# A two-layer encoder on one core: other order of the first loads, squares of x placed after its copies, group sums by transposes, the last sum in two runs

## The chip, the cores and the metric

The kernel runs on one core of a Trainium2 chip. Its engines are TensorE (PE, with PEld for its weight loads), VectorE (DVE), ScalarE (ACT), GpSimd (POOL) and SyncE (SP), each with its own in-order queue; sixteen DMA engines move data between memory and the chip. The metric is the device time of one execution in microseconds (us), lower is better. The median of three runs before the change is 617.97 us (617.78 to 618.43).

## The reference, cut to what matters

Two layers work on x of 256 tokens by 1024 features, all in float32. A layer is a mixer and then a channel part:

```python
h = rms_norm(x, n1)
proj = h @ w_in_l                      # 1024 x 2560: q, k, v of three kinds of heads
out_a = neighbourhood_attention(...)   # 4 heads
out_d = dilated_window_attention(...)  # 6 heads
out_c = gqa_block_attention(...)       # 6 heads, 2 of keys and values
mix = concat(rms_norm(out_a), rms_norm(out_d), rms_norm(out_c))
x = x + mix @ w_out_l
h = rms_norm(x, n2)
g, u = split(h @ w_gu)                 # 2 x 2816
x = x + (gelu(conv3(g)) * u) @ w_dn
```

`rms_norm` divides a row by the root of its mean square. The division is by one number for a token, so it can be taken after a product with weights.

## The kernel before, in words

**Numbers.** A float32 product is taken in three products of a faster format. An operand is split into a high part (a cast, by ScalarE) and a low part (what the cast left, by VectorE); `mm3` (line 610) adds high x high, high x low and low x high in PSUM. In profile names `wp_raw` is a piece of weights as loaded, `wp_hi` and `wp_lo` its parts, `act_hT` the turned x with its two parts side by side, `psa` and `psw` PSUM tiles of one bank each, four of either kind, and `act_s2k` a scratch tile with many uses. x lives in `const_x` (128 partitions, two halves t of 128 tokens, 1024 features); a block of x is 128 features of both halves.

**Weights.** They are streamed in units of at most 1 MB through four raw tiles and two pairs of part tiles (`load`, 561; `split`, 584; `unit`, 599). The first projection, "dq", needs two units of 768 KB: unit 0 holds feature blocks 0 to 3, unit 1 blocks 4 to 7. Unit 0 is loaded in four slices of one block, mixed with x, the gains of the norms, and the identity that transposes need; the list `START` (45) gives the queue and the order of these loads. Unit 1 is loaded in two halves, later units in one piece each.

**The start.** `gains_T` (506) transposes the gains. `split(0)` casts unit 0's slices. `split_T` (623) transposes x by TensorE, two blocks to a PSUM tile, and for each block ScalarE writes the high part times the gain and VectorE the low part. Then come the projections (802); `mean_squares` (647) has ScalarE square x in four pieces of 128 x 512 with the sum over a row as a by-product, and GpSimd turn the sums into the mean and its root. The mean is first needed when the heads of "dq" are normed (875), once "dq" is summed. Matmuls on a constant tile (`warm`, 512 to 524) fill TensorE's time before the weights are there.

**Group sums.** Each of the three groups of heads is normed over its features, which after attention lie on the partitions. `mixed` (1032) adds up the squares in a 128 x 256 tile; `group_rstd` (1047) sums them over the partitions by a matmul with a column of ones, copies the 128 x 2 result to SBUF and takes the root. `out_projections` (826) has VectorE scale the product with `w_out` by it and add it to x. There are three such sums a layer, after the sixth head, the twelfth and the last one.

**The end.** `down` (1308) adds the steps of the last product into four PSUM tiles `dacc[t][h]` of 128 x 512, one for each half of tokens and of features. The last two steps are taken together: for each of the four tiles, 12 matmuls of 512 columns, 6 a step. VectorE then scales each tile, adds it to x, and in the last layer SyncE stores the piece.

**What sets the order.** The program does not run in the order in which it is written. All operations are first recorded by `Plan` (220) with what they depend on. `order` (301) then simulates the engines with a price for each operation (`cost`, 414), a price for handing over from engine to engine, and one for loads (lines 384 to 392), and always takes the operation that can begin first; of two that can begin at once, the one of lower rank. The rank is the place in the text plus what `later(n)` adds. `not_before(engine)` (245) makes operations depend on the last one recorded so far on that engine. The engines' queues are written in the order so found. For dependencies a PSUM tile counts as a whole bank whatever part is used (`footprint`, 130):

```python
if self.tile.pool.psum:
    return (0, P, ((0, BANK),))
```

All operations are issued from line 411, so the profile's groups have to be told apart by their tiles.

Of the kernel before, what the change touches and what calls it, by code (L numbers as in the profile page):

```python
# [11 lines left out]
F32 = mybir.dt.float32  # L12
# [33 lines left out]
    ("act", "x", (0, 1)), ("sync", "g", 0), ("act", "x", (1, 1)), ("sync", "ident", 0), ("sync", "w", 0),  # L46
# [8 lines left out]

SPLIT_LATER, TURN_LATER, MIX_LATER, PREP_LATER = 50, 100, 100, 30
# [163 lines left out]
class Plan:  # L220
# [80 lines left out]
    def order(self):  # L301
# [49 lines left out]
        while len(done) < len(ops):  # L351
# [102 lines left out]
def encoder_kernel(  # L454
# [76 lines left out]
    ones = const.tile([P, 1], F32, tag="ones", name="ones")  # L531
    nc.gpsimd.memset(ones, 1.0)
# [257 lines left out]
    for l in range(DEPTH):  # L790
# [60 lines left out]
        me, rx = mean_squares(f"n1{l}")  # L851
# [195 lines left out]
        def group_rstd(gi):  # L1047
# [259 lines left out]

        def down(steps):
            ws = [unit() for _ in steps]
            for h in range(2):  # L1310
                hs = slice(h * 512, (h + 1) * 512)
                for t in range(NT):
                    c = slice(t * P, (t + 1) * P)
                    for s, (wh, wl) in zip(steps, ws):
# [104 lines left out]
```

## Time and profile before

| | |
|---|---|
| median of three runs | 617.97 us (617.78 to 618.43) |
| the profiled execution's own time | 617.81 us |
| its span, from first to last instruction | 616.0 us |
| TensorE, VectorE, ScalarE busy | 98%, 79%, 70% of the span |
| granted TensorE clock, mean | 0.999 |
| moved by DMA | 104.66 MB, 170 GB/s in the mean |

The span is what the trace covers; the time holds 1.8 us more around it. A row of instructions gives its start and its length, the engine, the line, the operation, output and inputs with their shapes, how many it merges, and in brackets how long the engine was idle before and what released it. A row of a group gives count, total busy time, mean in ns, and the idle time before. The row of a chain of waits gives the start, the length and what ran. Matmuls are pipelined: one row's length includes the time through the array, so the pace is read from start to start. ScalarE's `ACTIVATION_READ_ACCUMULATOR` is the second half of a square with a sum.

### The profile page before, as it was taken

To read this page: it belongs to the slowest core of one execution; us is meant where nothing else is said; L and a number is where in the kernel's file an instruction comes from. 1 tells how busy PE (TensorE), PEld (TensorE's weight loads), DVE (VectorE), ACT (ScalarE), POOL (GpSimd) and SP (SyncE) were. 2 spreads that over 40 slices of the span, in tenths; PEclk is the share of its full clock that TensorE was granted. 3 is DMA by queue.
4 is the path that set the end of the run, shared out by engine and by line. 5 is a ranking of instruction groups with operands and counts; after the bars stand their busy time and mean duration, and the time that the engine had idled before them with its cause. 6 is when DMAs were issued, how large, how long until landed. Compare 5 with 4: busy or idle time off the path is not lost.

```text
span 616.0 us, 9844 instructions
## 1 busy us (share of the span) xinstructions
PE 606.0 (98%) x3496; PEld 524.8 (85%) x3496; DVE 485.8 (79%) x1000; ACT 428.8 (70%) x1064; POOL 77.4 (13%) x125
## 2 busy tenths in 40 slices
PE   8999999999999999999999999999999999999997
PEld 6999878888888888888899989887888888888886
DVE  4898988897877877777867798979877777777775
ACT  6888989686566565556588899897756565566551
POOL 2731230211500000000023212112000000000000
PEclk9999999999999999999999999999999999999999
DMA  8894311755596555655444632127575555555501
GB/s 284 274 291 146 103 38 37 245 195 197 183 231 222 178 197 204 199 169 162 155 148 150 233 104 86 34 73 243 182 238 173 191 205 186 169 192 204 168 40 68
DMA packets 81617, 104.66 MB, mean 170 GB/s; under 512 B 9480, under 2 KB 69224, under 8 KB 81568
## 3 DMA queue, kind: packets, MB, share of 16 engines
q1 hardware_dynamic: 81024, 103.78, 52.0%
q8 instruction: 27, 0.44, 0.3%
q10 hardware_dynamic: 544, 0.26, 0.1%
q14 instruction: 22, 0.18, 0.1%
HBM read 102.54 MB, written 1.49 MB: 169 GB/s over the span
## 4 chain that ended last, share of the span: by engine, by line
PE 93%; ACT 3%; DVE 2%; DMA 1%; issue 1%; SPq 0%; ACTq 0%; DVEq 0%
PE psw_w L411 49%; PE psa_a L411 44%; ACT act_s2k L411 2%; DMA wp_raw<-in_w_in_dram 1%; DVE act_hT L411 1%; DVE wp_lo L411 1%; DVE const_x L411 0%; ACT wp_hi L411 0%; ACT act_hT L411 0%; ACT act_ch L411 0%; SPq L411 0%; DVE act_cl L411 0%; DVE act_z L411 0%; ACT const_v L411 0%; DVE small_nm L411 0%
## 5 line engine op out<-in xcount | busy, mean ns | idle before, releaser
L411 DVE TENSOR_TENSOR wp_lo<-wp_raw,wp_hi 128x512 fp32r<-128x512 f32 (+2 forms) x348 | 243.9, 729 | 49.7 <-ACT wp_hi L411 47.8
L411 PE MATMUL psw_w<-act_hT,wp_hi 128*128 128x512 f32 x704 | 247.6, 397 | 2.0 <-DVE act_hT L411 2.0
L411 ACT CAST wp_hi<-wp_raw 128x512 fp32r<-128x512 f32 (+2 forms) x348 | 212.7, 660 | 29.3 <-PE psw_w L411 15.6
L411 PE MATMUL psw_w<-act_hT,wp_lo 128*128 128x256 f32 x704 | 195.7, 279 | 0.0
L411 PEld LDWEIGHTS psw_w<-act_hT,wp_hi 128*128 128x128 f32 x704 | 131.8, 188 | 34.1 <-DVE act_hT L411 3.2
L411 PEld LDWEIGHTS psw_w<-act_hT,wp_lo 128*128 128x128 f32 x704 | 132.6, 188 | 1.2
L411 PE MATMUL psa_a<-wp_hi,act_hT 128*128 128x384 f32 (+2 forms) x448 | 113.1, 333 | 1.3 <-ACT act_hT L411 1.2
L411 ACT COPY act_s2k<-psw_w 128x256 f32<-128x256 f32 x88 | 32.3, 372 | 80.2 <-PE psw_w L411 80.2
L411 PEld LDWEIGHTS psa_a<-wp_hi,act_hT 128*128 128x128 f32 x448 | 77.9, 189 | 4.5 <-ACT act_hT L411 1.6
L411 PE MATMUL psa_a<-wp_lo,act_hT 128*128 128x384 f32 (+2 forms) x224 | 74.6, 334 | 0.0
L411 PE MATMUL psa_a<-wp_lo,act_ch 128*128 128x512 f32 x176 | 69.5, 395 | 0.0
L411 PE MATMUL psa_a<-wp_hi,act_ch 128*128 128x512 f32 x176 | 69.3, 394 | 0.0
L411 PE MATMUL psa_a<-wp_hi,act_cl 128*128 128x512 f32 x176 | 66.1, 394 | 0.0
L411 DVE TENSOR_TENSOR act_s2k<-psw_w,act_s2k 128x256 f32<-128x256 f32 x88 | 36.8, 422 | 32.4 <-ACT act_s2k L411 31.9
L411 PEld LDWEIGHTS psa_a<-wp_lo,act_hT 128*128 128x128 f32 x224 | 42.2, 189 | 1.9 <-DVE wp_lo L411 1.0
L411 PEld LDWEIGHTS psa_a<-wp_hi,act_cl 128*128 128x128 f32 x176 | 33.2, 188 | 7.7
L411 PEld LDWEIGHTS psa_a<-wp_hi,act_ch 128*128 128x128 f32 x176 | 33.1, 188 | 7.8
L411 PEld LDWEIGHTS psa_a<-wp_lo,act_ch 128*128 128x128 f32 x176 | 33.1, 188 | 6.9
L411 DVE SCALAR_TENSOR_TENSOR act_s2k<-act_s2k,act_cw,act_s2k 128x255 f32<-128x255 f32 x88 | 36.7, 476 | 1.4 <-ACT act_s2k L411 1.3
L411 POOL TENSOR_TENSOR small_rstd<-small_ms,const_mh 128x6 f32<-128x6 f32 (+2 forms) x26 | 32.0, 1232 | 2.2
L411 ACT ACTIVATE act_s2k<-act_s2k,act_cw 128x256 f32<-128x256 f32 x44 | 24.1, 595 | 11.6 <-DVE act_s2k L411 11.6
L411 PE MATMUL psw_w<-act_ch,const_v 128*128 128x256 f32 x128 | 28.5, 287 | 1.6 <-ACT act_s2k L411 1.1
(109 smaller groups left out, 754.3 us busy)
## 6 DMA issues: line engine op xcount, KB each, us to landing
wp_raw<-in_w_gate_up_dram SPq DMA_DIRECT2D x44, 1024.0 KB, 5.0
wp_raw<-in_w_down_dram SPq DMA_DIRECT2D x22, 1024.0 KB, 4.8
wp_raw<-in_w_in_dram SPq DMA_DIRECT2D x14, 768.0 KB, 5.9
wp_raw<-in_w_in_dram SPq DMA_DIRECT2D x8, 1024.0 KB, 5.9
wp_raw<-in_w_out_dram SPq DMA_DIRECT2D x8, 768.0 KB, 4.3
wp_raw<-in_w_out_dram SPq DMA_DIRECT2D x4, 512.0 KB, 3.8
act_nab<-dram_scr SPq DMA_DIRECT2D x4, 448.0 KB, 7.0
out_dram<-const_x SPq DMA_DIRECT2D x4, 256.0 KB, 2.0
```

Source lines behind the costliest of these rows:

```text
L411: getattr(o.engine.real, o.method)(*map(real, o.args), **{k: real(v) for k, v in o.kw.items()})
```

## The change

The list of the first loads is altered: the gains of the first norm come on ScalarE's queue in place of x's block 1, which goes to SyncE's queue behind the first slice of weights. x is copied in runs of 1, 1, 2 and 4 blocks in the first layer, the first run ahead of `split(0)`, whose operations depend on it. The four squares of the first layer depend on the last of those copies and have 50 added to their rank. The planner's prices for the first loads are altered. `group_rstd` transposes the two 128 x 128 halves of the squares and sums over the columns, instead of a product with ones. In the last layer the last of the four tiles is summed in two runs of 256 columns, with two sums and two stores. The second layer's start keeps its order of operations.

```diff
 START = [
-    ("act", "x", (0, 1)), ("sync", "g", 0), ("act", "x", (1, 1)), ("sync", "ident", 0), ("sync", "w", 0),
+    ("act", "x", (0, 1)), ("act", "g", 0), ("sync", "ident", 0), ("sync", "w", 0), ("sync", "x", (1, 1)),
     ("sync", "w", 1), ("sync", "x", (2, 2)), ("sync", "w", 2), ("sync", "w", 3), ("sync", "x", (4, 2)),
     ("sync", "x", (6, 2)), ("sync", "g", 1), ("sync", "g", 2),
 ]
+SQUARES_LATER = 50
...
+    def last_of(self, engine):
+        return max(i for i, o in enumerate(self.ops) if o.engine.name == engine)
-    def not_before(self, engine):
-        self.behind = max(i for i, o in enumerate(self.ops) if o.engine.name == engine)
+    def not_before(self, engine, at=None):
+        self.behind = self.last_of(engine) if at is None else at
...
-                end = max(end + 900, wires.get(ring, 0.0))
+                early = i < self.first_loads
+                end = max(end + (350 if early else 900), wires.get(ring, 0.0))
                 shared = 0.0
-                if i < self.first_loads:
-                    shared = o.size if ring == "ACT" else min(o.size, 120 * max(0.0, wires.get("ACT", 0.0) - end))
-                wires[ring] = end + shared / 120 + (o.size - shared) / (280 if i < self.first_loads else 360)
-                end = wires[ring] + 900
+                if early:
+                    shared = o.size if ring == "ACT" else min(o.size, 110 * max(0.0, wires.get("ACT", 0.0) - end))
+                wires[ring] = end + shared / (150 if ring == "ACT" else 110) + (o.size - shared) / (280 if early else 360)
+                end = wires[ring] + (1700 if early else 900)
...
-    ones = const.tile([P, 1], F32, tag="ones", name="ones")
-    nc.gpsimd.memset(ones, 1.0)
...
-    def mean_squares(name):
+    def mean_squares(name, behind=None):
...
-                nc.scalar.activation(
-                    junk, xs[:, t, h * 512 : (h + 1) * 512], AF.Square, accum_out=ss[:, t, h : h + 1]
-                )
+                with nc.not_before("ACT", behind) if behind else nullcontext():
+                    nc.scalar.activation(
+                        junk, xs[:, t, h * 512 : (h + 1) * 512], AF.Square, accum_out=ss[:, t, h : h + 1]
+                    )
...
-            split(0)
-        for h in range(2):
-            split_T(halves(h), hT_hi, hT_lo, 4 * h, gains[:, 0, l, 4 * h : 4 * h + 4], f"n1{l}{h}")
+        for b, n in [(0, 1), (1, 1), (2, 2), (4, 4)] if l == 0 else [(0, 4), (4, 4)]:
+            srcs = [xs[:, t, b * P : (b + n) * P] for t in range(NT)]
+            split_T(srcs, hT_hi, hT_lo, b, gains[:, 0, l, b : b + n], f"n1{l}{b}")
+            if l + b == 0:
+                with nc.not_before("ACT"):
+                    split(0)
+        turned_x = nc.last_of("ACT")
...
-        me, rx = mean_squares(f"n1{l}")
+        with nc.later(SQUARES_LATER if l == 0 else 0):
+            me, rx = mean_squares(f"n1{l}", turned_x if l == 0 else None)
...
-                nc.tensor.matmul(
-                    ps[:, t : t + 1], hold["sq", gi][:, t * P : (t + 1) * P], ones, start=True, stop=True
-                )
+                cols = slice(t * P, (t + 1) * P)
+                nc.tensor.transpose(ps[:, cols], hold["sq", gi][:, cols], ident)
-            nc.vector.tensor_copy(ss, ps[:, :NT])
+            nc.vector.reduce_sum(ss, ps[:, :S].rearrange("p (t d) -> p t d", d=P), axis=AX.X)
...
+        ends = whole = [(h, t, 0, 512) for h in range(2) for t in range(NT)]
+        if l == DEPTH - 1:
+            ends = whole[:-1] + [(1, NT - 1, 0, 256), (1, NT - 1, 256, 256)]
+
         def down(steps):
             ws = [unit() for _ in steps]
+            for h, t, c0, n in ends if STEPS - 1 in steps else whole:
+                hs, os = slice(h * 512 + c0, h * 512 + c0 + n), slice(c0, c0 + n)
...
+                            dacc[t][h][:, os], ch[:, j, c], cl[:, j, c], wh[:, j, hs], wl[:, j, hs],
+                            s == 0 and j == 0, s == STEPS - 1 and j == 1 and c0 + n == 512,
...
+        for h, t, c0, n in ends:
+            hs = slice(h * 512 + c0, h * 512 + c0 + n)
+            nc.vector.scalar_tensor_tensor(
+                xs[:, t, hs], dacc[t][h][:, c0 : c0 + n], r2[:, t : t + 1], xs[:, t, hs], ALU.mult, ALU.add
+            )
+            if l == DEPTH - 1:
+                nc.sync.dma_start(ov[:, t, hs], xs[:, t, hs])
```

More of the change, by code (lines that the diff above doesn't have):

```diff
@@ L2 @@
 import re
-from contextlib import ExitStack, contextmanager
+from contextlib import ExitStack, contextmanager, nullcontext
 import numpy as np
@@ L1306, in up @@
             ready[s] = (ch, cl)
+        ends = whole = [(h, t, 0, 512) for h in range(2) for t in range(NT)]
+        if l == DEPTH - 1:
+            ends = whole[:-1] + [(1, NT - 1, 0, 256), (1, NT - 1, 256, 256)]
         def down(steps):
             ws = [unit() for _ in steps]
[L1310 to L1314, printed above, removed]
-                        ch, cl = ready[s]
-                        for j in range(2):
-                            mm3(
-                                dacc[t][h], ch[:, j, c], cl[:, j, c], wh[:, j, hs], wl[:, j, hs],
-                                s == 0 and j == 0, s == STEPS - 1 and j == 1,
-                            )
+            for h, t, c0, n in ends if STEPS - 1 in steps else whole:
+                hs, os = slice(h * 512 + c0, h * 512 + c0 + n), slice(c0, c0 + n)
+                c = slice(t * P, (t + 1) * P)
+                for s, (wh, wl) in zip(steps, ws):
+                    ch, cl = ready[s]
+                    for j in range(2):
+                        mm3(
+                            dacc[t][h][:, os], ch[:, j, c], cl[:, j, c], wh[:, j, hs], wl[:, j, hs],
+                            s == 0 and j == 0, s == STEPS - 1 and j == 1 and c0 + n == 512,
+                        )
         last = []
```

9 lines of the change are left out of this document (1 added, 8 removed).

## The prediction

> **What bounds the kernel now.** I read the page first, then a table of stages, then the chain of waits, and last the single instructions of the places that the diff touches. From the page, the span, the busy shares and the chain by engine:
>
> ```profile
> span 616.0 us, 9844 instructions
> PE 606.0 (98%) x3496; PEld 524.8 (85%) x3496; DVE 485.8 (79%) x1000; ACT 428.8 (70%) x1064; POOL 77.4 (13%) x125
> ...
> PE 93%; ACT 3%; DVE 2%; DMA 1%; issue 1%; SPq 0%; ACTq 0%; DVEq 0%
> ```
>
> TensorE makes up 93% of the chain, so an edit can pay only where PE waits or by taking work off PE. Three stages (start:end, length, busy time of PE, PEld, DVE, ACT, POOL, granted clock, DMA share, GB/s) show where it waits; the rest is nearly full:
>
> ```profile
> 0.00:15.00 15.00, 12.69 (x74) 9.90 (x75) 6.74 (x17) 9.93 (x25) 3.96 (x14) 1.00 0.86 281
> 80.00:130.00 50.00, 47.40 (x304) 39.70 (x303) 42.86 (x102) 41.06 (x113) 12.85 (x17) 1.00 0.32 104
> 400.00:450.00 50.00, 48.51 (x287) 40.78 (x286) 43.15 (x96) 39.33 (x92) 6.47 (x10) 1.00 0.52 171
> ```
>
> PE idles 2.31 us in the first, 2.60 and 1.49 in the two around the ends of the layers' attention. The change reaches all three, and the last microseconds.
>
> **The start as it is.** The chain of waits of the first 30 us, cut to what matters, and two stretches, the second and third of the first projection's matmuls alone:
>
> ```profile
> 1.63 4.46 DMA wp_raw<-in_w_in_dram
> ...
> 6.11 0.52 ACT wp_hi L411
> ...
> 8.01 1.32 ACT act_s2k L411 x4
> 9.33 0.82 ACT wp_hi L411 x2
> ...
> 11.61 0.61 ACT act_s2k L411 x2
> ...
> 12.95 0.61 ACT act_s2k L411 x2
> ...
> 14.01 14.85 PE psa_a L411 x81
> ```
>
> ```profile
> 6.00:14.00 8.00, 6.84 (x42) 5.80 (x42) 5.57 (x14) 7.65 (x22) 0.27 (x2) 1.00 1.03 349
> ...
> 7.00:14.00 7.00, 5.24 (x24) 1.00 1.03 350
> 14.00:18.50 4.50, 4.49 (x24) 1.00 0.98 272
> ```
>
> The first weights land at 6.09. From 6 to 14 ScalarE is busy 7.65 of 8.00 us and sets the pace: it casts four slices of weights, copies x's eight blocks, and squares x in between (the act_s2k rows), 1.32 + 0.61 + 0.61 = 2.54 us on the chain. By 14.0 PE has done 24 of the first projection's 48 matmuls; from 14.01 it is dense, the other 24 taking 4.49, 0.187 each.
>
> **Part 1, the loads.** SyncE's first issues, and the GB/s of the first 8 us in forty slices:
>
> ```profile
> 1.18 0.41 SPq L411 DMA_DIRECT2D const_ident<-in_c_ident_dram  x1
> 1.63 0.91 SPq L411 DMA_DIRECT2D wp_raw<-in_w_in_dram  x2
> ```
>
> ```profile
> GB/s 0 0 0 0 0 0 0 0 15 115 253 246 310 233 241 159 197 187 200 261 307 346 269 243 261 243 202 279 264 289 315 320 382 359 358 376 361 374 374 387
> ```
>
> x's blocks 0 and 1, the gains, the identity and the first slice (131 + 131 + 8 + 66 + 197 KB) are 533 KB; the row adds up to that at 4.2 us, and the slice lands 1.9 us later. With block 1 behind it, 402 KB go ahead, reached at 3.7, and the slice takes the identity's slot, 0.45 us sooner. Estimate: landing at 5.5, the first matmul at 6.3 (7.04 now). Block 1 lands as the last of the 533 KB, at 6.1, just before its use. Block 0's copy, now in a PSUM tile of its own and ahead of the casts, waits only for block 0 and the gains, and the gains now come on ScalarE's queue, which issues two loads as before: nothing. SyncE's queue loses one issue (the gains) and takes one (block 1), so from blocks 2 and 3 on the bytes and slots ahead are the same and nothing behind lands earlier.
>
> **Part 2, the squares** go behind the last copy. ScalarE's copies and casts of this stretch are then done at 13.43 - 2.54 = 10.9 by ScalarE's own work, and two other things are late next: arrivals and PE itself.
>
> ```profile
> DMA packets 2158, 2.84 MB, mean 355 GB/s; under 512 B 128, under 2 KB 2158, under 8 KB 2158
> ```
>
> ```profile
> 13.43 3.01 ACT L411 CAST wp_hi<-wp_raw 128x384 fp32r<-128x384 f32 x7
> 18.33 0.28 POOL L411 TENSOR_SCALAR small_ms<-small_ss,small_he 128x6 f32<-128x6 f32 x1 [2.77 <-ACT act_s2k L411]
> 22.98 1.76 ACT L411 CAST wp_hi<-wp_raw 128x384 fp32r<-128x384 f32 x4 [1.55 <-DMA wp_raw<-in_w_in_dram]
> ...
> 14.00:23.00 9.00, 8.99 (x50) 8.70 (x51) 6.87 (x16) 7.07 (x36) 5.81 (x10) 1.00 1.03 325
> ```
>
> x, the first unit, the identity and the gains are 1.05 + 0.79 + 0.07 + 0.02 = 1.93 MB; the second unit's halves (0.39 each) end at 2.32 and 2.71. 1.75 MB have moved at 8.0 (the sum of the row above), then 355 GB/s (the first row here, 8 to 16 us); with the 1.9 us they land at 11.5 and 12.6. PE went dense 0.58 after the cast of 13.43 began, so arrivals allow 12.1. But PE must first do 24 matmuls and 16 transposes from 6.3 on: 24 x 0.187 + 16 x 0.11 (0.11 is worked out in part 3) = 6.3, so 12.6. I take 12.6: **-1.4 us**. Bounds: -1.9 by arrivals, and +0.8 if the squares come before the casts (x lands 1.9 us after 1.93 MB, at 10.4; its last copies end at about 11.7, an estimate, and 11.7 + 2.54 is 0.8 behind 13.43).
>
> The squares' 2.54 us need a cover: between 14 and 23 ScalarE works 7.07 of 9.00, so 1.93 are free, and the stretch begins 1.4 earlier; 0.8 remain. Queued behind them are the casts for the second projection and the sums of the first one's heads; and GpSimd's mean of x, which had 2.77 us to spare before it was used, loses about that much. The cast at 22.98 waits for a transfer and does not move; PE needs it at 14.01 + 72 x 0.183 = 27.2 now, 25.8 then, so this cover holds.
>
> **Part 3, the group sums**, six of them. Old sum and next transpose, two runs of transposes, the two kinds of read, and a wait on the read:
>
> ```profile
> 419.05 0.50 PE L411 MATMUL psw_w<-const_ones,act_sqm 128*128 128x1 f32 x4
> 419.41 0.27 PE L411 MATMUL psw_w<-const_ident,act_s2k 88*128 88x88 f32 x1
> ...
> 121.14 0.38 PE L411 MATMUL psw_w<-const_ident,const_x 128*128 128x128 f32 x2
> ...
> 121.83 0.82 PE L411 MATMUL psw_w<-const_ident,const_x 128*128 128x128 f32 x6
> ...
> 90.60 0.77 PEld L411 LDWEIGHTS psw_w<-act_kc,act_qc 64*128 64x128 f32 x12 [0.36 <-DVE small_ss L411]
> ```
>
> ```profile
> L411 DVE TENSOR_REDUCE small_nm<-psw_w 128x1 f32<-128x256 f32 x24 | 8.7, 416 | 2.5 <-PE psw_w L411 1.8 <-ACT act_s2k L411 0.6
> ...
> L411 DVE COPY small_ss<-psw_w 128x2 f32<-128x2 f32 x6 | 0.9, 155 | 0.5 <-PE psw_w L411 0.3
> ```
>
> The four old records take 0.36 from start to start; transposes (0.82 - 0.38) / 4 = 0.11 each, two 0.22. PE saves 0.14 a sum. The read grows from 0.155 to about 0.416 (nearest row: a reduction over as many columns), +0.26, so the result is 0.12 later. At the sum of 90 us PE waits for that read: +0.12. The last group of each layer feeds the sum into x that PE's transposes wait for: the saving goes into that wait, 0. The other three: -0.42. Together **-0.3 us**; bounds 6 x -0.14 = -0.84, and 6 x +0.26 = +1.6. The memset of the ones, ahead of all work on GpSimd, is worth nothing.
>
> **Part 4, the last sum.** TensorE's pace by width, a case of a PSUM bank written in two parts, two widths of the sum, and the end:
>
> ```profile
> 143.33 5.56 PE psa_a L411 x24
> 148.90 11.29 PE psw_w L411 x64
> ...
> 380.85 0.97 PE L411 MATMUL psw_w<-act_kc,act_qc 64*128 64x256 f32 x12
> 381.86 0.76 DVE L411 TENSOR_REDUCE small_nm<-psw_w 128x1 f32<-128x256 f32 x2 [0.26 <-PE psw_w L411]
> ...
> 123.58 1.65 DVE L411 SCALAR_TENSOR_TENSOR act_hT<-psw_w,const_gains,act_hT 128x256 fp32r<-128x256 f32 x4
> ...
> 612.41 0.75 DVE L411 SCALAR_TENSOR_TENSOR const_x<-psa_a,small_rx,const_x 128x512 f32<-128x512 f32 x1 [0.65 <-PE psa_a L411]
> ...
> 613.19 0.33 SPq L411 DMA_DIRECT2D out_dram<-const_x  x1
> ```
>
> ```profile
> GB/s 0 0 0 0 0 0 0 0 0 0 0 0 358 369 369 215 215 379 410 287 21 0 0 328 379 379 226 0 0 0 338 379 369 226 0 0 0 0 0 0
> ```
>
> 512 columns take 5.56 / 24 = 0.232; the run of 64 is half 512 and half 256 wide, so 256 take (11.29 - 32 x 0.232) / 32 = 0.12: splitting is free on PE (24 x 0.12 against 12 x 0.232, +0.1). Does the first half's sum start before the second half's matmuls end? The reduction at 381.86 reads columns whose six matmuls are the first of the twelve, and starts after all twelve: the program orders by whole banks. So both sums follow PE's end: 2 x 0.41 = 0.83 (1.65 / 4) instead of 0.75. The last issue is 0.08 later, its data, four slices of 0.2 us now (608 us + the row's slices), half as long: -0.35; **-0.25 us**. Bounds: -0.65 if the halves are tracked apart (0.75 - 0.41 and the 0.35), +0.15 if 1 KB rows move at half the rate.
> The Trainium skill (PSUM — Partial Sum Buffer, "PSUM bank collisions raise a hardware error") says the same of any engine pair: guard by bank, a different address in the bank still collides. The trace agrees (0.26 us of wait at 381.86); by address the end would be 0.4 better, by bank -0.25.
>
> **Part 5, the planner's new load prices** move no work themselves, but the whole order is written anew from them: valued at 0; this is the last rival.
>
> **The sum** against the profiled execution's own 617.81 (span 616.0 and 1.8 around it; the runs' median is 617.97): 617.81 - 1.4 - 0.3 - 0.25 = **615.9**.
>
> **Rivals.**
> (1) All at its better bound: -1.9 - 0.84 - 0.65 gives 614.4. For it: the stages are full of PE work. Against: the wait at 381.86.
> (2) The start's gain is taken back: ScalarE, with 0.8 us left, hands over the second projection's casts late, or the landing at 22.98 comes later because transfers fill the queue (DMA share 1.03 to 23 us). Leaves -0.3 of the start: 617.81 - 0.3 - 0.3 - 0.25 = 617.0. Against: 1.4 us between landing and use.
> (3) PE's clock falls in the gap between the warm-up and the first matmul:
>
> ```profile
> 0.98 3.25 PE L411 MATMUL psw_w<-const_warm 128*128 128x256 bf16 x15 [0.98 <-POOL const_warm L411]
> ```
>
> Those first fifteen took 0.217 each, against 0.12 for 256 columns later. A second such stretch loses 3.25 x (1 - 0.12 / 0.217) = 1.45: 617.3. Against: the gap shrinks, and the granted clock is 1.00 throughout.
> The Trainium skill (TensorE: Matmul & The Clock Gate, "What's actually happening") has the clock halve after one idle window of about 3.4 us; no gap here comes near, so by that rule it stays up.
> (4) Slower: the new order costs in the attention. Place: the stages 80:130 and 400:450, where PE already idles 4.09 us; a group's read or a head's copy queued one place worse stops PE, whose queue is in order. Doubled, 617.81 - 1.95 + 4.09 = 620.0; it decides from 6.04 us of idle time there, twice the present one being 8.18. For it: every order after the start depends on times that move. Against: durations and hand-overs of that part are priced as before, and the chain is PE's, unbroken, for 81 matmuls from 14.01.
>
> **How the numbers follow.** Forecast 0.58 (its own range 614.9 to 616.8), rivals 0.09, 0.18, 0.04 and 0.11. A measurement of this kernel can tell 0.2%, 1.2 us, from no change. Faster by more than that is below 616.7: most of the forecast, (1), and some of (2), 0.69; within it the rest of (2), (3) and the edges, 0.21; slower 0.10. The range 614.4 to 617.6 takes in (1), (2) and (3) and leaves (4) out.
>
> **What would show it.** Right: the first weight cast near 5.5; no squares among the copies; PE dense at 12.6; PE idle under 1.2 us between 7 and 14; six pairs of transposes with reductions near 0.42; two final sums after PE's end, the last issue at the same distance from it. Wrong: casts of the second unit behind squares, a PE wait on wp_hi or wp_lo between 14 and 30, or more than 6 us idle in the two attention stages.

## The result and the profile after

The changed kernel takes **622.93 us** (median of 4 runs, 622.65 to 623.44) against 617.88 us (617.77 to 618.43) before: ratio 1.008, 95% interval 1.0068 to 1.0091. It is slower by 5 us. The forecast was 615.9 us.

The page of the changed kernel (span and instructions, busy times, the chain by engine), and the same three stages as in the prediction:

```profile
span 621.7 us, 9849 instructions
...
PE 606.2 (98%) x3496; PEld 524.8 (84%) x3496; DVE 487.9 (78%) x1001; ACT 429.6 (69%) x1064; POOL 80.1 (13%) x124
...
PE 90%; ACT 4%; DVE 3%; POOL 2%; issue 1%; DVEq 0%; POOLq 0%; ACTq 0%
```

```profile
0.00:15.00 15.00, 12.86 (x75) 10.15 (x75) 6.90 (x16) 8.58 (x20) 2.73 (x10) 1.00 0.89 281
80.00:130.00 50.00, 48.56 (x324) 41.20 (x323) 44.53 (x104) 43.42 (x119) 10.32 (x15) 1.00 0.35 120
400.00:450.00 50.00, 46.45 (x279) 38.78 (x278) 42.02 (x90) 38.16 (x91) 7.30 (x10) 1.00 0.47 159
```

TensorE has the same work (606.2 us, 606.0 before), but its share of the chain fell from 93 to 90%: others stop it more. The first 15 us are no worse; the end of layer 0's attention (80 to 130) gained 1.2 us of PE's time, that of layer 1 (400 to 450) lost 2.1. Together TensorE idles 1.44 + 3.55 = 4.99 us in these two, under the 6.04 from which the prediction's rival (4) was to be taken. The 5 us are in none of the three stages.

To find them I laid milestones along the chain of waits, rows that both kernels have: the turn of the first projection (A), the first matmuls of layer 0's channel part (B) and of layer 1's (D), the sum behind TensorE's end (L), the end of the span (S). The rows of the changed kernel, then those of before that the prediction doesn't show:

```profile
34.21 0.65 PE psw_w L416 x6
...
147.25 5.58 PE psa_a L416 x24
...
450.18 5.58 PE psa_a L416 x24
```

```profile
28.86 0.66 PE psw_w L411 x6
...
444.86 5.58 PE psa_a L411 x24
```

| us | A | A to B | B to D | D to L | L to S |
|---|---|---|---|---|---|
| before | 28.86 | 114.47 | 301.53 | 167.55 | 3.59 |
| after | 34.21 | 113.04 | 302.93 | 167.61 | 3.91 |
| difference | **+5.35** | **-1.43** | **+1.40** | +0.06 | **+0.32** |

The differences add up to the 5.7 us between the spans. By these intervals the loss lies in the first 34 us; the gain in layer 0 and the loss in layer 1 cancel. And it isn't in the first 14: counts of matmuls of the projections alone, before and after, show the changed kernel 31 - 26 = 5 matmuls ahead at 14 us, 0.9 us at 0.187 each. (Two matmuls in flight at 12.6 count in both rows: started by 14 are 24 before and 29 after.)

```profile
6.00:12.60 6.60, 4.46 (x21) 1.00 1.02 350
12.60:14.00 1.40, 0.78 (x5) 1.00 1.04 349
```

```profile
6.00:12.60 6.60, 4.98 (x22) 1.00 1.05 370
12.60:14.00 1.40, 1.40 (x9) 1.00 1.07 376
```

From 14 to 35 us, before and then after (PE, PEld, DVE, ACT, POOL, clock, DMA share, GB/s), TensorE does 92 matmuls instead of 120:

```profile
14.00:35.00 21.00, 20.99 (x120) 20.28 (x121) 17.93 (x40) 17.61 (x84) 17.13 (x30) 1.00 0.91 301
```

```profile
14.00:35.00 21.00, 17.68 (x92) 15.96 (x91) 13.14 (x29) 14.29 (x74) 12.89 (x19) 0.92 0.78 246
```

It idles 3.3 us there and runs at a granted clock of 0.92. The single instructions (start, length, in brackets the idle time before and what ended it) show how:

```profile
17.96 1.38 ACT L416 CAST wp_hi<-wp_raw 128x384 fp32r<-128x384 f32 x3
...
25.87 1.83 POOL L416 COPY act_nab<-act_few 28x1984 f32<-28x1984 f32 x1
...
25.76 0.56 DVE L416 TENSOR_TENSOR act_z<-psa_a,small_rstd 128x384 f32<-128x384 f32 x1 [1.22 <-POOL small_rstd L416]
26.24 1.87 DVE L416 TENSOR_TENSOR wp_lo<-wp_raw,wp_hi 128x384 fp32r<-128x384 f32 x1
...
22.34 0.44 PE L416 MATMUL psa_a<-wp_lo,act_hT 128*128 128x384 f32 x1 [0.80 <-DVE wp_lo L416]
...
28.17 0.69 PE L416 MATMUL psa_a<-wp_lo,act_hT 128*128 128x384 f32 x1 [2.41 <-DVE wp_lo L416]
```

TensorE waits twice for a low part of the weights. It also loses time that isn't counted as idle: with the casts of the third piece of weights, which the second projection begins with, not started before 17.96, it runs on the constant tile.

```profile
17.84 0.61 PE L416 MATMUL psw_w<-const_warm 128*128 128x256 bf16 x4
18.57 0.62 PE L416 MATMUL psa_a<-wp_hi,act_hT 128*128 128x384 f32 x2
```

At 18.57 the second projection begins; in the kernel before it follows the first without a gap at 18.53, so the lead of 0.9 us is gone here. Before the second wait VectorE waits 1.22 us for a norm's factor, and then the low part takes 1.87 us where others take 0.55. At its end the clock falls (columns as above):

```profile
26.00:29.00 3.00, 0.83 (x3) 0.83 (x4) 3.00 (x6) 0.00 (x0) 1.69 (x1) 0.82 0.09 34
29.00:32.00 3.00, 3.00 (x13) 3.00 (x12) 2.33 (x6) 1.51 (x13) 0.06 (x1) 0.61 0.50 160
```

The chain leads from this wait back through VectorE, both factors and the mean of x on GpSimd to the squares on ScalarE (2.46 us from 14.43). That was my first reading (the squares are late, so the mean is, so all behind it). The experiments did not bear it out.

This profile is of the one execution of four whose mean clock was below 1.000 (0.997, 623.44 us). The other three took 622.65 to 622.94, so the clock isn't what the 5 us are made of, though it adds to the 5.35 at A.

### The profile page after: what moved, and what is told of

It is laid out like the page before. It is cut to its first block, busy times and chain, and to the rows that moved or that the text cites. A ratio compares the mean times of both kernels' runs of the same rounds, so it can differ in the third digit from the quotient of the medians.

```text
span 621.7 us, 9849 instructions
## 1 busy us (share of the span) xinstructions
PE 606.2 (98%) x3496; PEld 524.8 (84%) x3496; DVE 487.9 (78%) x1001; ACT 429.6 (69%) x1064; POOL 80.1 (13%) x124
## 4 chain that ended last, share of the span: by engine, by line
PE 90%; ACT 4%; DVE 3%; POOL 2%; issue 1%; DVEq 0%; POOLq 0%; ACTq 0%
PE psw_w L416 49%; PE psa_a L416 41%; ACT act_s2k L416 2%; POOL small_rstd L416 1%; DVE const_x L416 1%; ACT wp_hi L416 1%; ACT act_hT L416 1%; DVE wp_lo L416 1%; POOL small_ms L416 1%; DVE act_hT L416 0%; DVE act_cl L416 0%; ACT L416 0%; DVE small_ss L416 0%; DVE act_mixT_lo L416 0%; DVE small_nm L416 0%
## 5 line engine op out<-in xcount | busy, mean ns | idle before, releaser
L416 PE MATMUL psa_a<-wp_lo,act_ch 128*128 128x512 f32 (+1 forms) x180 | 70.1, 390 | 0.0
L416 PE MATMUL psa_a<-wp_hi,act_ch 128*128 128x512 f32 (+1 forms) x180 | 70.1, 389 | 0.0
L416 PE MATMUL psa_a<-wp_hi,act_cl 128*128 128x512 f32 (+1 forms) x180 | 66.8, 389 | 0.0
```

The source lines that it names most:

```text
L416: getattr(o.engine.real, o.method)(*map(real, o.args), **{k: real(v) for k, v in o.kw.items()})
```

## The experiments

### Each part undone

The same four intervals for every kernel below, from the same rows (one profile for each; the two with a star lost some 1.5 us from B to D to the clock, told further down; "-": the chain of that profile does not pass there):

| | time, us | ratio to before, 95% | A | A to B | B to D |
|---|---|---|---|---|---|
| squares back in place | 618.98 | 1.0015 to 1.0036 | 29.38 | 112.77 | 302.96 |
| sums by ones again | 623.59 | 1.0078 to 1.0108 | 34.59 | 114.16 | 301.23 |
| last sum in one run | 624.26 | 1.009 to 1.0121 | 34.62 | 113.04 | 303.28 |
| early small activation | 623.45 | 1.0075 to 1.0109 | 32.26 | 113.10 | 303.20 |
| GpSimd: norms first | 623.9 | 1.0078 to 1.0105 | - | - | 302.93 |
| mean from a constant* | 623.2 | 1.0067 to 1.0102 | 33.39 | 113.05 | 304.74 |
| no squares | 618.88 | 1.0008 to 1.0026 | 29.09 | 113.09 | 303.15 |
| squares behind third piece | 620.2 | 1.0031 to 1.0071 | - | - | 303.22 |
| squares of 16 columns* | 623.35 | 1.0069 to 1.0103 | 31.99 | 113.03 | 304.75 |
| copy of 62 elements | 621.41 | 1.0045 to 1.0077 | 31.38 | 113.04 | 302.84 |
| before, transposes, order kept | 618.63 | 0.9996 to 1.0014 | 28.80 | 114.44 | 302.24 |
| before, transposes in layer 0 | 617.11 | 0.9978 to 0.9995 | 29.00 | 113.39 | 301.49 |
| several parts, see the end | 616.9 | 0.9971 to 0.9988 | 29.19 | 112.93 | 301.53 |

**Squares back**, all else as changed.

```diff
-        with nc.later(SQUARES_LATER if l == 0 else 0):
-            me, rx = mean_squares(f"n1{l}", turned_x if l == 0 else None)
+        me, rx = mean_squares(f"n1{l}")
```

> The changed kernel with one part undone: the squares of x are recorded as before, free to run between the copies. Theory S (the late squares make the mean late on GpSimd, its roots late, VectorE waits for them in order with the low parts of the weights behind, and PE starves between 17 and 30 us; this is where 5.35 of the 5.0 to 5.7 us went): the turn of the first projection, at 28.86 before and 34.21 after, comes back to 28.5 to 29.8, and the time to 617.0 to 618.8. Theory R (the order of the whole program was written anew and costs in both attention parts, whatever the squares do): above 621.

618.98 us: 4.0 of the 5 us are gone, A is at 29.38. The place of the squares costs the time. What is left of the start, loads, order of the copies and the planner's new load prices, is 0.5 us behind before at A.

**Sums by ones.**

```diff
-                nc.tensor.transpose(ps[:, cols], hold["sq", gi][:, cols], ident)
+                nc.tensor.matmul(ps[:, t : t + 1], hold["sq", gi][:, cols], ones, start=True, stop=True)
...
-            nc.vector.reduce_sum(ss, ps[:, :S].rearrange("p (t d) -> p t d", d=P), axis=AX.X)
+            nc.vector.tensor_copy(ss, ps[:, :NT])
```

> The changed kernel with one part undone: the groups' squares are summed by products with a column of ones again, with the short copy. Theory S: the start is untouched, so 621.5 to 623.5. Theory G (the longer reads lie on the chain at the ends of the attention, at 416.39 and 424.88 us, 0.27 each, and the waits behind them add up to the 1.7 us lost there): 620.8 to 621.5.

The time can't be told from that of the changed kernel (the intervals overlap), but by stages two effects cancel: A to B is 1.1 us longer without the transposes, B to D 1.7 shorter.

**One run at the end.**

```diff
-        if l == DEPTH - 1:
-            ends = whole[:-1] + [(1, NT - 1, 0, 256), (1, NT - 1, 256, 256)]
```

> The changed kernel with one part undone: the last sum in one run of 512 columns. From PE's end to the span's end there are 3.94 us in the changed kernel and 3.61 in the one before. If that belongs to the two runs: 622.6, and 3.6 us in its profile; if the two runs gain as forecast: 623.2.

The time is not lower, since its start was worse (34.62) and B to D 0.35 longer. The end itself is shorter, L to S 3.57 instead of 3.91:

```profile
617.79 0.88 DVE L416 SCALAR_TENSOR_TENSOR const_x<-psa_a,small_rx,const_x 128x256 f32<-128x256 f32 x2 [1.37 <-PE psa_a L416]
618.30 0.81 SPq L416 DMA_DIRECT2D out_dram<-const_x  x2
```

```profile
618.83 0.75 DVE L416 SCALAR_TENSOR_TENSOR const_x<-psa_a,small_rx,const_x 128x512 f32<-128x512 f32 x1 [0.65 <-PE psa_a L416]
619.61 0.33 SPq L416 DMA_DIRECT2D out_dram<-const_x  x1
```

With two runs (first fence) both sums follow TensorE's end, and two issues of 0.4 us follow each other. With one, the single issue starts 0.78 us after the sum's start, and the span ends 2.8 us after the issue began (622.4 - 619.61); with two the second issue starts at about 618.7 and the end is 3.0 later (621.7). Half the data did not end sooner. That the first of the two stores stands in its way is not ruled out.

**An early small activation**: behind `load(0)`

```diff
+    early = const.tile([P, 1], F32, tag="early", name="early")
+    nc.scalar.copy(early, minus_half[:, 0:1])
```

> The changed kernel with one operation more: a copy of one column by ScalarE, recorded right after the first loads. ScalarE's table load starts at 4.82 in the changed kernel and at 1.72 before, because its first operation that needs a table now waits for the gains. Theory T (this takes the start's gain): the table load returns to about 2, the first matmul comes at 6.2 to 6.5 instead of 7.04, and the time falls by 0.5 to 0.9, to 622.0 to 622.4. Theory S alone (the roots set PE's pace): the same as far as the squares come earlier, which is also at most 0.9; if arrivals of x set the squares, no change, 622.9.

```profile
4.82 1.28 ACT L416 ACT_TABLE_LOAD   x1 [4.82 <-DVE const_gains L416]
6.12 0.47 ACT L416 ACTIVATE act_hT<-psw_w,const_gains 128x256 fp32r<-128x256 f32 x1
...
7.04 0.62 PE L416 MATMUL psa_a<-wp_hi,act_hT 128*128 128x384 f32 x2 [0.88 <-ACT wp_hi L416]
```

```profile
1.72 1.28 ACT L416 ACT_TABLE_LOAD   x1 [1.72 <-issue]
...
6.43 0.62 PE L416 MATMUL psa_a<-wp_hi,act_hT 128*128 128x384 f32 x2
```

The first fence is the changed kernel, the second this one. In the changed kernel ScalarE's first activation is x's first copy, which needs the gains, and the load of its function table stands behind the same wait, at 4.82; that puts the first matmul at 7.04, as before the change. With an earlier activation that needs nothing the load runs at 1.72 and the first matmul at 6.43. The same two waits are there, but 0.5 us sooner (0.80 us ending at 21.82, 2.42 us ending at 27.64). The median did not follow: three of its four executions ran at a clock of 0.996 to 0.997. The one at 1.000 took 621.85 us, where the changed kernel took 622.65 to 622.94 at 1.000, so some gain is likely and not shown.

### Why the place of the squares costs 4 us

**GpSimd's order.** In the changed kernel GpSimd builds the tables of k ahead of the second factor, and the copy of the bias right behind it. Here the factors go first, tables and copy behind:

```diff
+            zs = [normed(pj["d" + which][t], H_DIL, t, f"d{which}{l}{t}") for t in range(NT)]
...
-                tables["d" + which, l] = tables_d(l, which)
+                with nc.not_before("POOL"):
+                    tables["d" + which, l] = tables_d(l, which)
...
-            na_repeat(0)
+            with nc.not_before("POOL"):
+                na_repeat(0)
```

> The changed kernel, squares late as in it, with GpSimd's order written out: both pairs of roots of the first projection before the products of tables, and the copy of the neighbourhood bias behind the second projection's roots. Theory S1 (what starves PE is GpSimd's queue, unbroken from 16.96 to 25.7 us with 1.8 us of table products ahead of the second pair of roots, and the copy that stretches a low part on VectorE from 0.55 to 1.87): the 2.41 us wait before 28.17 goes, the turn of the first projection comes at 30.5 to 32 instead of 34.21, the granted clock stays 1.00, time 619.0 to 621.0. Theory S2 (ScalarE's backlog of squares ahead of the casts is enough by itself): within 1 us of 622.9.

623.9 us: no gain. The wait of 2.41 us is gone, but others stand elsewhere (0.82 us at 20.8 on a cast, 1.59 us at 39.25 on a low part, behind a step of VectorE's that stood beside the copy). The profiled execution also lost some 1.5 us in the first 12 us, to the clock, but its executions at 0.999 and 1.000 took 623.28 and 623.78 us, no less than the changed kernel. So GpSimd's order alone, put right, gains nothing: the waits move.

**The mean from a constant, the order kept.**

```diff
+        if behind:
+            ss = small.tile([P, NT, 2], F32, tag="ssk", name=f"ssk_{name}", bufs=1)
+            nc.gpsimd.memset(ss, 512.0)
```

> The changed kernel with its four squares of layer 0 still on ScalarE at 14.3 to 16.9 us, but GpSimd takes the mean of x in layer 0 from a constant set ahead (the sums of squares are computed and not used). The order of every queue stays as in the changed kernel; only GpSimd's wait for the squares is gone. Backlog theory (what costs is that the squares and the first norm's sums stand on ScalarE ahead of the casts of the third piece of weights): the casts still start at about 17.96 us, TensorE still waits for the second parts of the weights at 22 and 28 us, its turn of the first projection stays at 33 to 34.3 us, the time at 621.5 to 623.5 us. Late-mean theory (what costs is that GpSimd begins the mean at 16.96 us and is unbroken from there): first norm's factor out at about 19.7 instead of 21.2 us, second at about 23.0 instead of 25.7 us, the wait at 28 us falls from 2.4 us to under 0.5 us, turn of the first projection at 29.5 to 31.5 us, time 618.5 to 620.5 us.

```profile
24.80 0.56 DVE L416 TENSOR_TENSOR act_z<-psa_a,small_rstd 128x384 f32<-128x384 f32 x1 [1.21 <-POOL small_rstd L416]
25.27 1.87 DVE L416 TENSOR_TENSOR wp_lo<-wp_raw,wp_hi 128x384 fp32r<-128x384 f32 x1
...
27.20 0.44 PE L416 MATMUL psa_a<-wp_lo,act_hT 128*128 128x384 f32 x1 [2.41 <-DVE wp_lo L416]
```

623.2 us. The wait of 0.80 us at 22.34 is gone and A comes 0.8 sooner, but the 2.41 us are there unchanged, 1 us earlier. The late mean is worth about 0.8 us of the 5.35 at A. As the main cause, my first reading falls.

**No squares, and squares one step later.**

```diff
+                if behind:
+                    continue
```

> The changed kernel without the four squares of x in layer 0: the mean of x in layer 0 is taken from a constant, so that work is left out. Both theories expect the lost start back: turn of the first projection at 27.5 to 29.5 us (34.2 in the changed kernel), time 616.5 to 618.5 us. If it stays over 31 us, neither the place of the squares nor the late mean is the cause, and it is the new order of the loads and of x's blocks.

```diff
+        if l == 0:
+            wv.until("dq")
-        with nc.later(SQUARES_LATER if l == 0 else 0):
-            me, rx = mean_squares(f"n1{l}", turned_x if l == 0 else None)
+        me, rx = mean_squares(f"n1{l}", nc.last_of("ACT") if l == 0 else None)
```

> The changed kernel with the squares of layer 0 one step later still: behind the casts of the third piece of weights instead of ahead of them, the mean of x behind them. Backlog theory: those casts run at about 14.3 instead of 17.96 us, TensorE loses none of the 0.5 us at 18 us and keeps a lead of one piece, turn of the first projection at 29 to 32 us, time 618 to 620.5 us. Late-mean theory: the mean comes another 1.5 us later (about 18.4 us), so the norm's factors and what is queued behind them do too: turn of the first projection at 34 to 36 us, time 622.5 to 625 us.

Without the squares (the mean is then taken from a constant) 618.88 us; with the squares later still, behind the casts of the third piece of weights, 620.2 us, 2.7 less than the changed kernel, though the mean is later (20.40 us against 16.96). In both the casts of the third piece come early:

```profile
14.88 1.34 ACT L416 CAST wp_hi<-wp_raw 128x384 fp32r<-128x384 f32 x3 [0.42 <-DMA wp_raw<-in_w_in_dram]
16.66 0.22 ACT L416 ACTIVATE act_s2k<-psa_a 128x64 f32<-128x64 f32 x1 [0.43 <-PE psa_a L416]
```

These are ScalarE's rows without the squares: the casts at 14.88 (17.96 in the changed kernel), and then the sums of the first norm, which can't start before 16.7 because TensorE is not through. So it goes with the casts, not with the mean. These two runs also have another order on GpSimd (without the squares the second factor is again ahead of the tables of k), so they don't show that the casts alone do it. And is it the 2.5 us that the squares take ahead of the casts?

**Squares of 16 columns, the order kept.**

```diff
+                    w = 16 if behind else 512
                     nc.scalar.activation(
-                        junk, xs[:, t, h * 512 : (h + 1) * 512], AF.Square, accum_out=ss[:, t, h : h + 1]
+                        junk[:, :w], xs[:, t, h * 512 : h * 512 + w], AF.Square, accum_out=ss[:, t, h : h + 1]
                     )
+                    nc.ops[-1].ns = 0.833 * 512 + 184
```

> The changed kernel with its squares of x in layer 0 cut from 512 columns to 16 (so the mean of x in layer 0 is taken over 32 columns, the rest of that work is left out), while the planner is told their old price, so that the order of every queue stays as in the changed kernel. Time theory (the 2.5 us that the squares take on ScalarE are what delays the casts behind them): without them the casts of the third piece start about 1.5 us sooner, turn of the first projection at 29 to 31 us, time 617.5 to 619.5 us. Order theory (the squares filled ScalarE's open time in the planner's reckoning, and the order written around them puts the first norm's sums, which wait for TensorE until about 16.7 us, ahead of the casts of the third piece, and GpSimd's tables ahead of the second norm's factor): the sums still end at about 17.9 us and the casts still start at about 17.9 us, a wait of 2 to 2.5 us of TensorE on the second parts of the weights stays at 27 to 28 us, turn of the first projection at 32.5 to 34 us, time 621.3 to 623.3 us.

```profile
16.91 0.23 ACT L416 ACTIVATE act_s2k<-psa_a 128x64 f32<-128x64 f32 x1 [1.43 <-PE psa_a L416]
...
18.11 1.37 ACT L416 CAST wp_hi<-wp_raw 128x384 fp32r<-128x384 f32 x3
...
27.36 0.44 PE L416 MATMUL psa_a<-wp_lo,act_hT 128*128 128x384 f32 x1 [2.40 <-DVE wp_lo L416]
```

623.35 us: **mainly the order, not the squares' time**. ScalarE now stands idle for 1.43 us, and the casts still start at 18.11, because they are queued behind sums that wait for TensorE. From there on TensorE has no weights in hand, and twice a low part is queued on VectorE behind a norm instruction that waits for GpSimd.

A is at 31.99, between what the two theories had expected, 2.2 us sooner than in the changed kernel. The wait of 0.80 us at 22.34 is gone with the late mean, and the clock held here in the start (1.00 from 26 to 32 us) and fell in layer 1 instead. At the same mean clock the times are the same: 622.59 to 623.38 in the four executions here (0.996 to 0.997), 623.44 in the changed kernel's profile (0.997).

Why the planner put the sums first can be read from the changed kernel's own `order`, which reckons without the chip. It has the four squares on ScalarE from 12.95 to 15.39 us and the casts of the third piece ready at 13.74. With the 50 added the squares have ranks 172 to 175, still below the casts' 184, so they go first whenever both can begin. At 15.39 the first norm's sums, rank 175 on, are reckoned to be ready too, and go ahead of the casts in their turn. Without the squares it starts the casts at 13.74, when no sum is ready. On the chip TensorE let the first sum start only at 16.91 in this run.

**GpSimd's copy cut, the order kept.**

```diff
+    nabs[0] = act.tile([P, RPB_C, GRID_W], F32, tag="nab", name="nab0", bufs=1)
+    nc.gpsimd.memset(nabs[0].rearrange("p r c -> p (r c)")[:NR], 0.0)
...
+        w = GRID_W if l else 2
         nc.gpsimd.tensor_copy(
-            rows_.rearrange("p (n c) -> p n c", c=RPB_C),
-            nabs["few"].unsqueeze(1).to_broadcast([NR, GRID_W, RPB_C]),
+            rows_.rearrange("p (n c) -> p n c", c=RPB_C)[:, :w],
+            nabs["few"].unsqueeze(1).to_broadcast([NR, w, RPB_C]),
         )
+        nc.ops[-1].ns = 3.4 * GRID_W * RPB_C
```

> The changed kernel with GpSimd's copy at 25.87 us (28x1984 elements, 1.83 us) cut to 28x62 elements, the rest of that tile set to zero at the start (so most of the bias of the neighbourhood attention in layer 0 is left out), with the order of every queue as in the changed kernel. Contention theory (the copy beside it is what makes VectorE's second part of the weights take 1.87 instead of 0.55 us): that instruction takes 0.5 to 0.7 us, TensorE's wait of 2.41 us at 28.17 us falls to 0.9 to 1.3 us, its clock stays at 1.00 after it, turn of the first projection at 31.5 to 33 us, time 620 to 621.7 us. Rival (that instruction is slow for another reason, or the wait is set by the norm's factor alone): it still takes over 1.5 us, or the wait stays over 2 us, turn of the first projection at 33.5 to 34.7 us, time 622.3 to 623.3 us.

```profile
25.65 0.56 DVE L416 TENSOR_TENSOR act_z<-psa_a,small_rstd 128x384 f32<-128x384 f32 x1 [1.21 <-POOL small_rstd L416]
26.12 0.55 DVE L416 TENSOR_TENSOR wp_lo<-wp_raw,wp_hi 128x384 fp32r<-128x384 f32 x1
...
26.73 0.44 PE L416 MATMUL psa_a<-wp_lo,act_hT 128*128 128x384 f32 x1 [1.09 <-DVE wp_lo L416]
```

621.41 us, A at 31.38. The low part takes 0.55 us, the wait is 1.09 instead of 2.41, and the clock stays at 1.00. Of the changed kernel's wait 1.3 us are VectorE standing beside GpSimd's copy; the rest is the wait for the factor. In the kernel before, the copy ran at the same stage (24.25 us there) and stretched two small instructions of VectorE's (128x48, 2.01 us for both, 0.34 elsewhere), but TensorE, with weights in hand, did not wait.

### The sums of the groups, and a faster kernel

Before and after differ in the operation of the sums and in the order that the planner writes for it. To part them, the kernel before with transposes and reductions at the planner's old prices, so that the order stays:

```diff
+                nc.tensor.transpose(ps[:, cols], hold["sq", gi][:, cols], ident)
+                nc.ops[-1].ns = 108
...
+            nc.vector.reduce_sum(ss, ps[:, :S].rearrange("p (t d) -> p t d", d=P), axis=AX.X)
+            nc.ops[-1].ns = 1.04 * NT + 70
```

> The kernel before with the group sums by transposes and reductions, priced in the planner as the old operations, so that every queue keeps the old order. Layer 1's attention, from the end of layer 0's last product to layer 1's first, takes 144.9 us with products by ones and 146.6 with transposes (in four kernels). Theory O (the longer reads on VectorE do this): 146 or more here, and the time 0 to 1.5 us longer than before. Theory P (the order that the planner writes for them does it): 144.5 to 145, and the time is 0 to 0.8 us shorter than before, by 0.14 us of PE at up to six sums.

618.63 us, no change that can be told: 0.0 in layer 0, +0.7 in layer 1, in one profile. No gain of the operation by itself can be seen. In every kernel where the order is written anew with them, layer 0 gains 1.1 to 1.7 us, and wherever they stand in layer 1 and the clock holds there, B to D is 1.3 to 1.8 longer. So the gain in layer 0 is the order's. Of the loss in layer 1 some 0.7 came with the operation here, and the rest with the order.

The kernel before with transposes in layer 0 alone, the order written anew:

```diff
-                nc.tensor.matmul(
-                    ps[:, t : t + 1], hold["sq", gi][:, t * P : (t + 1) * P], ones, start=True, stop=True
-                )
+                cols = slice(t * P, (t + 1) * P)
+                if l == 0:
+                    nc.tensor.transpose(ps[:, cols], hold["sq", gi][:, cols], ident)
+                else:
+                    nc.tensor.matmul(ps[:, t : t + 1], hold["sq", gi][:, cols], ones, start=True, stop=True)
```

and the read likewise.

> The kernel before, with nothing changed but the sums of squares of the groups in layer 0, which are transposed and added on VectorE instead of multiplied by ones; the order of the work is written anew for it. If layer 0's gain of 1.1 to 1.7 us (from the turn of the first projection to the first work of the feed-forward, 114.5 before and 112.8 to 113.1 with the changed sums in the kernels that differ from the changed one) comes with the new order whatever the start, 616.2 to 617.0 us, ratio 0.997 to 0.9987. If it needs the changed start's own order, 617.7 to 618.2 us, ratio 0.9995 to 1.0005.

617.11 us, ratio 0.9986 (0.9978 to 0.9995): the gain in layer 0 (1.1 us) comes with the old start too, though the time is 0.1 us above what was expected.

The parts that had gained put together: the changed loads with the squares in place, the early activation, transposes in layer 0 alone, one run at the end; that is, the changed kernel with the first, third and fourth of the edits above and this one for layer 1 only:

```diff
+                if l == 0:
+                    nc.tensor.transpose(ps[:, cols], hold["sq", gi][:, cols], ident)
+                else:
+                    nc.tensor.matmul(ps[:, t : t + 1], hold["sq", gi][:, cols], ones, start=True, stop=True)
```

> A mixture: the new loads and copies, the table load brought forward by a first copy, squares where they were, transposes in layer 0 only, the last sum in one run. By the stretches measured so far against the kernel before: start +0.52 with the late table load and 0.6 less without, layer 0 -1.7, layer 1 0, end 0: 615.7 to 616.6. If the planner's orders do not carry over from kernel to kernel: 617 to 619.

616.9 us, ratio 0.9979 (0.9971 to 0.9988): 1.3 us less than the kernel before beside it (618.24), and short of the 615.7 to 616.6 expected. It isn't told apart from the one edit above; A is still 0.3 us later than before, so the gain is layer 0's.

## Why the prediction was wrong

The forecast was 617.81 - 1.4 - 0.3 - 0.25; the profiled execution of the changed kernel took 623.44. The error sits in the first term: -1.4 for the start, where A came 5.35 us later. The prediction's own sign of being wrong, a wait on `wp_lo` between 14 and 30 us, is there twice (0.80 and 2.41).

**Part 1, -0.7 at the first matmul: not had.** The step "block 0's copy ... waits only for block 0 and the gains ...: nothing" failed. As ScalarE's first activation it draws the function table's load (1.28 us) behind its own wait. The first matmul stayed at 7.04. With the table loaded early it is at 6.43, where I had 6.3.

**Part 2, -1.4: 0.9 was there, and was lost with 5 us more.** The 24th matmul was forecast for 12.6; 22 had started by then, 29 by 14.0 (21 and 24 before). With the squares back 24 had started by 14.0, so squares off ScalarE's path did bring a lead. What failed is the cover: "ScalarE works 7.07 of 9.00, so 1.93 are free ...; 0.8 remain". It counts ScalarE's time, and the run with squares of 16 columns shows that time is not the main matter: with 1.43 us idle on ScalarE the casts start no sooner (18.11 against 17.96) and the time is the same. What I named as queued behind the squares, the casts and the sums, has an order, and the planner turned it round. The sentence "GpSimd's mean ... loses about that much" was about right in size (it begins 3.3 us later, 16.96 against 13.64) and worth about 0.8 us.

**Rival (2)** had the right place, "hands over the second projection's casts late", and a wrong price: it let the start's gain go and no more. The waits that followed cost 3.3 us of idle time and a clock of 0.92. Its point of decision was put at a spare time of ScalarE, not at the order.

**Rival (3)**, the clock, was held at 0.04 for the gap before the first matmul. There it fell in one profile (the last section), and in the changed kernel it fell at the end of the second wait. It is a price of the waits, not a way of its own: executions of the changed kernel with a mean granted clock of 1.000 still took 622.65 to 622.94.

**Rival (4)**, 620.0, was right about the mechanism and wrong about the place: the order costs, but in the start. In the attention stages it gave 1.43 us in layer 0 and took 1.40 up to layer 1's channel part.

**Part 3, -0.3: about 0.** The durations were right:

```profile
L416 DVE TENSOR_REDUCE small_ss<-psw_w 128x2 f32<-128x256 f32 x6 | 2.5, 418 | 0.1
```

0.418 us against 0.416 forecast. The step that TensorE's saving of 0.14 a sum shows in the time failed: with the order kept the operation gains 0.0 in layer 0 and loses 0.7 in layer 1.

**Part 4, -0.25: +0.3.** Both sums follow TensorE's end, as worked out, and the last issue comes about 0.15 us later where I had 0.08. "Its data ... half as long: -0.35" failed: issue to end is 3.0 us with half the data and 2.8 with all of it.

**Part 5, "valued at 0"**, is where the prediction named the rewritten order, and the order was worth more than all other parts. The new load prices alone did not do it: the run with the squares back keeps them and is 0.5 us behind at A. No run took back the prices by themselves.

## What to carry to other kernels

Where a planner writes the order from prices, moving one operation is a change to every queue: price it by what ends up behind what, above all where work that waits for another engine ends up ahead of work that feeds the bottleneck. Spare time of an engine is no cover when its queue is in order. To learn whether an operation's time or its place in the order costs, shrink it while telling the planner the old price.

## What was not expected of the hardware

**The clock can fall after short gaps.** In the same place of layer 1, a gap of 1.6 us left the clock up in the profile of the changed kernel, and in that with squares of 16 columns the clock fell behind it (the matmul behind the gap, and two stretches with clock, DMA share and GB/s at their end):

```profile
430.84 0.50 PE L416 MATMUL psw_w<-act_hT,wp_hi 128*128 128x512 f32 x1 [1.59 <-DVE act_hT L416]
...
428.00:432.00 4.00, 2.19 (x14) 1.65 (x13) 3.93 (x9) 4.00 (x12) 0.00 (x0) 1.00 0.55 214
432.00:436.00 4.00, 2.99 (x21) 2.54 (x20) 3.71 (x7) 3.35 (x9) 1.85 (x3) 1.00 0.42 130
```

```profile
428.89 0.50 PE L416 MATMUL psw_w<-act_hT,wp_hi 128*128 128x512 f32 x1 [1.60 <-DVE act_hT L416]
...
428.00:432.00 4.00, 3.11 (x11) 2.68 (x12) 3.93 (x9) 3.81 (x10) 1.48 (x3) 0.68 0.08 30
432.00:436.00 4.00, 2.99 (x18) 2.51 (x17) 2.17 (x5) 1.57 (x4) 0.37 (x1) 0.90 0.81 262
```

That cost 1.5 us (B to D 304.75 against 302.8 to 303.3). In the profile with GpSimd's norms first the gap before the first matmul was 1.38 us, and the granted clock was 0.50 from 8 to 10 us; the same gap of 1.38 us left it at 1.00 in three other profiles (squares back, no squares, mean from a constant). So the length of the gap alone doesn't decide it. Each fall in these profiles is 3.41 us at a granted clock of 0.50 (27.91 to 31.32 us in the changed kernel, 429.40 to 432.81 with squares of 16 columns). This parts executions of one kernel: the early activation took 621.85 us at a mean clock of 1.000 and 623.3 to 623.7 at 0.996 and 0.997. The Trainium skill (TensorE: Matmul & The Clock Gate, "What's actually happening") has the clock halve after an idle window of about 3.4 us. The gaps of 1.38 and 1.6 us are less than half of that, and the 2.41 us of the changed kernel are short of it too, so here the measurement differs from the rule as I used it in the prediction.

**VectorE beside GpSimd's copy.** The low part that began during the copy (25.87 to 27.70) took 1.87 us and ended at 28.11, 0.4 after it; without the copy 0.55. The Trainium skill (SBUF — State Buffer, "SBUF: two separate sides") has the two engines share a port pair that one holds for its whole instruction, against a VectorE instruction with two SBUF inputs too, when GpSimd's reads SBUF, as this copy does. The trace agrees.

**A table load inherits the wait** of the first activation (4.82 against 1.72 us), and in one pair of profiles **a last store of 128 KB, right behind another, ended no sooner after its issue than one of 256 KB** (3.0 and 2.8 us).
